# A two-layer encoder on one core: rows scaled before they are turned, and another order of loads in the opening

## The chip, the cores and the metric

One NeuronCore of one Trainium2 chip runs the whole program in one launch. The metric is the device time of an execution in microseconds (us). TensorE (PE) multiplies and turns tiles, VectorE (DVE) and ScalarE (ACT) work on elements, SyncE (SP) issues the loads from DRAM, GpSimd (POOL) does a few memsets.

## The reference, cut to what matters

Two sequences, 1024 rows ("sample") and 256 rows ("prompt") of 1024 features, go through two layers with the same weights. Only the start of the first layer matters here:

```python
for i in range(DEPTH):
    mod = jax.nn.silu(c) @ w_ada[i] + b_ada[i]
    sh1, sc1, g1, sh2, sc2, g2 = jnp.split(mod[:, None, :], 6, axis=-1)
    h = rms_norm(x, norm_g[i, 0]) * (1 + sc1) + sh1
    ...                                   # GLA mixer: q, k, v, r, gates from h
    x = x + g1 * rms_norm(y, norm_g[i, 1])
    h = rms_norm(x, norm_g[i, 2]) * (1 + sc2) + sh2
    ...                                   # SwiGLU FFN
def rms_norm(x, g):
    return x * lax.rsqrt(jnp.mean(x * x, axis=-1, keepdims=True) + EPS) * g
def gla_mixer(h, w_in, w_gk1, ...):
    q, k, v, r = jnp.split(h @ w_in, ...)
    gate = jnp.einsum('bld,edr->eblr', h, w_gk1)
    ...
```

## The kernel before, in words

The rows are cut into three blocks: C (the 256 prompt rows), A and B (512 sample rows each). Everything is fp32; a product is made in three passes over a rounded part and a remainder (`hhi`/`hlo` for activations, `uhi`/`ulo` for weights), and the activations stand with the features on the partitions, as eight pieces `k` of 128 features.

The opening stage runs from the start of the program to the loop over heads. Its parts, with the names used below:

- `rows1`/`rows2`: seven small loads (conditioning vectors, norm gains, biases), turned by PE into `vec1`/`vec2`; `sct` is silu of the conditioning vectors.
- `load_x` (L657, L662, L663) loads tiles of 128 rows (`xtok`, 512 KB), PE turns each in eight 128x128 transposes, and DVE or ACT copies the turned halves from PSUM into `xt`.
- `squares`, `rstd_of`, `newton` (L443 to L465): squares of the turned block summed over the eight pieces on DVE, a matmul with `ones_d` that sums over partitions, and a Newton step on the block's whole width give `r`, the reciprocal root of each row's mean square, in every partition.
- `ada_group` (L338, L348): the shift and scale vectors come from `w_ada`, in two halves of four pieces each. A half needs eight loads of 512 KB (`wada`) and two matmuls per load. `ada_out` (L394, L412, L422, L430) brings the sums into `mods`.
- `apply_norm` (L481, L482, L492): per piece `u` = `xt` x scale x `r` (DVE), `hhi` = round(`u` + shift) (ACT), `hlo` = `u` + shift - `hhi` (DVE).
- `products`: the gate rank products (`gk1`, L734, L735) and the first head's q and k (`mm3`, L307 to L309) of C and A, in two halves that follow the two halves of `mods`. Later `vproj` (L322) makes the first head's values of C and A, while `norm_b` squares, scales and splits block B; then come `gk1` and q, k of B, and the values of B (L322 at 108.17 us).

Three things set the order. Each engine has one stream of instructions, written out by a scheduler in the build from the program's order, the data and its own times; on the chip an engine that waits holds up all behind it. SP's stream is the queue of the loads. And a load needs a free buffer: `rawp` has three of 512 KB for row tiles and weights, `up` five `uhi` and five `ulo`, which `wada` shares with split weights.

Of the kernel before, what the change touches and what calls it, by code (L numbers as in the profile page):

```python
# [8 lines left out]
F32 = mybir.dt.float32  # L9
# [3 lines left out]
ALU = mybir.AluOpType  # L13
# [4 lines left out]
KD = 8  # L18
# [20 lines left out]
def encoder_kernel(  # L39
# [400 lines left out]
    def sq_add(acc, a, k, p):  # L440
        n = a.shape[-1]
        if k == 0:
            act.activation(acc, a, AF.Square)  # L443
        else:
            sq = p.tile([128, n], F32, tag="sq", name=nm("sq"))
            act.activation(sq, a, AF.Square)
            dve.tensor_add(acc, acc, sq)

    def rstd_of(acc, n, p, ones=ones_d, exp=False):
        ms = ps_ax()[:, :n]  # L450
        pe.matmul(ms, lhsT=ones, rhs=acc, start=True, stop=True)
        return newton(ms, n, p, exp)
# [15 lines left out]
    def col(md, v, cd, k):  # L468
        return md[:, v, cd, k : k + 1]

    last_hi = [None]

    def apply_norm(blk, L, first, xt, r, keep=None, ks=range(KD)):
        n, cd, f = BLK[blk], COND[blk], BLK[blk] / 512
        md = mods[L]
        vsh, vsc = (0, 1) if first else (3, 4)
        last = None
        for k in ks:
            sh = col(md, vsh, cd, k)
            u = xt[:, k, :] if keep is None else keep.tile([128, n], F32, tag="u", name=nm("u"))  # L480
            dve.scalar_tensor_tensor(out=u, in0=xt[:, k, :], scalar=col(md, vsc, cd, k), in1=r, op0=ALU.mult, op1=ALU.mult)  # L481
            last_hi[0] = act.activation(hhi[blk][:, k, :], u, AF.Identity, bias=sh)  # L482
            yield 0.66 * f
            if last is not None:
                lo_part(blk, *last)
                yield 0.66 * f
            last = (k, u, sh)
        lo_part(blk, *last)
        yield 0.66 * f

    def lo_part(blk, k, u, sh):
        dve.scalar_tensor_tensor(  # L492
            out=hlo[blk][:, k, :], in0=u, scalar=sh, in1=hhi[blk][:, k, :].bitcast(F32), op0=ALU.add, op1=ALU.subtract,
        )


    def square_sum(to, a):
        act.activation(bt.tile([128, 512], F32, tag="sq", name=nm("sq")), a, AF.Square, accum_out=to)
# [1 line left out]
    def sums_tile(blk, tag):  # L500
        return bt.tile([128, BLK[blk] // 128, 2], F32, tag=tag + blk, bufs=1, name=nm("ss"))

    def rstd_tok(ss):
        nt = ss.shape[1]
        m, r, t = [bt.tile([128, nt], F32, tag=x, name=nm(x)) for x in ("m", "rt", "tt")]
# [4 lines left out]
        dve.tensor_mul(t, m, t)  # L510
        dve.tensor_scalar(t, t, -0.5, 1.5, ALU.mult, ALU.add)
        dve.tensor_mul(r, r, t)
        return r
# [113 lines left out]
        vs[blk] = v  # L627

    with tc.tile_pool(name="st", bufs=1, reuse_waits="tile") as st:
        rows1 = st.tile([98, 128], F32)  # L630
        rows2 = st.tile([96, 128], F32)
        ngr = norm_g.rearrange("l s (k p) -> (l s k) p", p=128)
        dma(out=rows1[V_C : V_C + 8, :], in_=c_sample.rearrange("a (k p) -> (a k) p", p=128))
        dma(out=rows1[V_C + 8 : V_C + 16, :], in_=c_prompt.rearrange("a (k p) -> (a k) p", p=128))
        dma(out=rows1[V_NG : V_NG + 64, :], in_=ngr)
        dma(out=rows1[V_GK : V_GK + 8, :], in_=gla_b_gk[0].rearrange("e (h p) -> (e h) p", p=128))
        dma(out=rows1[V_SGB : V_SGB + 8, :], in_=sg_b_in[0, 0:1024].rearrange("(k p) -> k p", p=128))
        dma(out=rows1[V_GH : V_GH + 2, :], in_=gla_g_head[0].rearrange("(k p) -> k p", p=128))
        dma(out=rows2, in_=b_ada.rearrange("l (k p) -> (l k) p", p=128))
        pt = ps_ax()  # L640
        pe.transpose(pt[:, 0:98], rows1, ident[:98, :98])
# [4 lines left out]
        act.activation(sct, vec1[:, V_C : V_C + 16].rearrange("p (c k) -> p c k", c=2), AF.Silu)  # L646

        xt = {}
        def load_x(blk, tiles=None, bank=ps_mm):
            n = BLK[blk]  # L650
            if blk not in xt:
                xt[blk] = st.tile([128, KD, n], F32, tag="xt" + blk, name=nm("xt"))
            t = xt[blk]
            s, o = src[blk]
            for i in tiles or range(n // 128):
                a = rawp.tile([128, D], F32, tag="raw", name=nm("xtok"))
                dma(out=a, in_=s[o + i * 128 : o + (i + 1) * 128, :])  # L657
                for hf in range(2):
                    ps = bank()
                    for j in range(4):  # L660
                        k = 4 * hf + j
                        pe.transpose(ps[:, j * 128 : (j + 1) * 128], a[:, k * 128 : (k + 1) * 128], ident)  # L662
                    (act.copy if hf or blk == "B" else dve.tensor_copy)(  # L663
                        t[:, 4 * hf : 4 * hf + 4, i * 128 : (i + 1) * 128], ps.rearrange("p (j t) -> p j t", j=4)
                    )

        class STP:
            def tile(self, shape, dt, tag, name):
                return st.tile(shape, dt, tag=tag, bufs=3 if tag == "r" else 2, name=name)

        stp = STP()

        accs = {}

        def norm_b():
            n = BLK["B"]
            acc = st.tile([128, n], F32, tag="accB", bufs=1, name=nm("acc"))
            for k in range(KD):
                sq_add(acc, xt["B"][:, k, :], k, stp)
                yield 0.6  # L680
            yield 0.6
            r = rstd_of(acc, n, stp)
            yield 2.3
            yield from apply_norm("B", 0, True, xt["B"], r, stp)

        def squares(blk):
            accs[blk] = st.tile([128, BLK[blk]], F32, tag="acc" + blk, bufs=1, name=nm("acc"))
            for k in range(KD):
                sq_add(accs[blk], xt[blk][:, k, :], k, stp)

        class ADP:
            i = 0
# [2 lines left out]
                self.i += 1  # L695
                return up.tile(shape, dt, tag=("uhi", "ulo")[self.i % 2], name=name)

        rs = {}
        adp = ADP()
        adas = [ada_group(0, (0, 1), adp, "wada", None, half=i) for i in range(2)]  # L700

        def ada_n(i, n=99):
            for _ in range(n):
                if next(adas[i], None) is None:
                    break
# [10 lines left out]
        act.copy(g1v[:, :, :, 2, :], g1v[:, :, :, 0, :].bitcast(F32))  # L716
        act.copy(g1v[:, :, :, 3, :], g1v[:, :, :, 1, :].bitcast(F32))

        load_x("C")
        ada_n(0, 2)  # L720
        load_x("A", [0, 1])
        squares("C")
        ada_n(0, 2)
        load_x("A", [2, 3])
        ada_n(0, 3)
        rs["C"] = rstd_of(accs["C"], BLK["C"], stp)
        squares("A")
        rs["A"] = rstd_of(accs["A"], BLK["A"], stp)
        ada_n(0)

        def gk1(ps, blk, ks=range(KD)):
# [28 lines left out]
                tick(us_, rate)  # L760

        halves = (range(0, 4), range(4, KD))
        acc_ps = {"C": [p[:, :256] for p in (ps_mm(False), ps_mm(False), ps_ax())], "A": [ps_so() for _ in range(2)]}

        def products(i, blk, n=0):
            ps = acc_ps[blk]
            gk1(ps[0], blk, halves[i])
            ada_n(1, n)
            for p, w in zip(ps[1:], (wq, wk)):
                mm3(p, w, blk, halves[i])  # L770
                ada_n(1, n)
            if i == 1:
                gk1_out(ps[0], blk)
                q_out(ps[1], blk)
                if blk == "A":
                    ps.append(ps_mm(False))
                    mm3(ps[2], wk, blk)
                k_out(ps[2], blk)

        def norm(blk, i):  # L780
            for _ in apply_norm(blk, 0, True, xt[blk], rs[blk], stp, halves[i]):
# [961 lines left out]
```

## Time and profile before

| | |
|---|---|
| median of 3 runs | 2790.86 us (2787.03 to 2794.0) |
| the profiled execution | 2796.02 us, span 2794.3 us |
| PE busy | 2724.6 us, 98% of the span |
| DVE, ACT, POOL busy | 1740.7, 1118.2, 32.6 us |
| DMA | 410.41 MB, mean 147 GB/s |
| mean granted TensorE clock | 0.990 |

The profile divides the span into 40 slices of 70 us, with tenths of busy time; 9 is 90% or more. PE is at 9 nearly everywhere: it is the bound of the program, and what is not busy lies at the start, at the end and in short waits. The opening stage is the first slice and a half.

### The profile page before, as it was taken

Reading aid. Unit: us, or ns where it says so; the run is one execution under the profiler, and the core shown is the slowest. Engines: PE = TensorE matmul, PEld = TensorE weight load, DVE = VectorE, ACT = ScalarE, POOL = GpSimd, SP = SyncE. Lnnn points to the kernel's source line nnn. Section 1 sums busy time; section 2 is a strip of 40 time slices with the busy share of each in tenths; the row PEclk is TensorE's granted clock in tenths of the full one; section 3 lists DMA queues with packets and bytes.
Section 4 is the critical chain, followed back from the end, with each engine's and each line's share of the span. In section 5 each row is a group of like instructions: output and inputs, shape, how many; then the busy total and the mean of one; then the engine's idle time right before and its main releaser. Section 6 shows DMA issues by size and latency. Waiting matters only on the chain.

```text
span 2794.3 us, 37049 instructions
## 1 busy us (share of the span) xinstructions
PE 2724.6 (98%) x14208; PEld 2280.7 (82%) x14208; DVE 1740.7 (62%) x2749; ACT 1118.2 (40%) x1892; POOL 32.6 (1%) x47
## 2 busy tenths in 40 slices
PE   7999999999999999999999999999999999999998
PEld 4887888977888788888778868887887888888886
DVE  6763646587865654447778578666856554445576
ACT  5442434444622223224357344425422232234443
POOL 0000000000000000000000000000000000000000
PEclk9999999999999999999999999999999999999999
DMA  6224232155255542237877342334355532237676
GB/s 231 68 67 149 74 110 69 54 177 180 96 165 172 180 138 76 96 97 259 267 245 240 125 158 77 121 125 148 100 166 176 187 98 92 79 115 260 195 235 210
DMA packets 317542, 410.41 MB, mean 147 GB/s; under 512 B 21058, under 2 KB 194820, under 8 KB 317364
## 3 DMA queue, kind: packets, MB, share of 16 engines
q1 hardware_dynamic: 317364, 408.04, 44.9%
q8 instruction: 111, 1.82, 0.3%
q14 instruction: 67, 0.55, 0.1%
HBM read 304.65 MB, written 103.32 MB: 146 GB/s over the span
## 4 chain that ended last, share of the span: by engine, by line
PE 73%; DMA 12%; DVE 10%; issue 2%; ACT 1%; SPq 1%; POOL 0%; DVEq 0%; ACTq 0%; POOLq 0%
PE pso L1260 11%; PE pmm L1260 5%; PE pmm L322 4%; DMA y<-in_ffn_w_out_dram 3%; PE pax L1260 3%; PE pso L1434 2%; PE pso L1435 2%; PE pso L1436 2%; DMA raw<-in_ffn_w_in_dram 2%; PE pmm L309 2%; PE pmm L308 2%; PE pmm L307 2%; PE pax L307 2%; PE pax L308 2%; PE pax L309 2%
## 5 line engine op out<-in xcount | busy, mean ns | idle before, releaser
L145 ACT CAST uhi<-raw 128x1024 fp32r<-128x1024 f32 (+1 forms) x299 | 307.5, 1030 | 640.6 <-issue 283.3
L146 DVE TENSOR_TENSOR ulo<-raw,uhi 128x1024 fp32r<-128x1024 f32 (+1 forms) x299 | 357.1, 1196 | 236.0 <-ACT uhi L145 231.9
L309 PE MATMUL pax<-hhiC,ulo 128*128 128x256 f32 x680 | 192.6, 283 | 0.0
L307 PE MATMUL pax<-hhiC,uhi 128*128 128x256 f32 x680 | 192.5, 283 | 0.0
L308 PE MATMUL pax<-hloC,uhi 128*128 128x256 f32 x680 | 192.4, 283 | 0.0
L1260 PE MATMUL pso<-t,uhi 128*128 128x512 f32 x428 | 150.4, 413 | 21.8 <-DVE c L1337 21.7
L1434 PE MATMUL pso<-uhi,hhiB 128*128 128x512 f32 x374 | 145.7, 390 | 1.0 <-DVE y L1417 1.0
L1435 PE MATMUL pso<-uhi,hloB 128*128 128x512 f32 x374 | 145.6, 389 | 0.0
L1436 PE MATMUL pso<-ulo,hhiB 128*128 128x512 f32 x374 | 145.5, 389 | 0.0
L307 PEld LDWEIGHTS pax<-hhiC,uhi 128*128 128x128 f32 x680 | 130.3, 192 | 3.8 <-ACT v L580 0.4
L308 PEld LDWEIGHTS pax<-hloC,uhi 128*128 128x128 f32 x680 | 130.2, 191 | 3.1
L309 PEld LDWEIGHTS pax<-hhiC,ulo 128*128 128x128 f32 x680 | 130.2, 191 | 1.7 <-issue 1.7
L1382 ACT CAST hhiB<-tl 128x512 fp32r<-128x512 f32 x154 | 94.5, 619 | 87.0 <-PE pso L1436 33.9
L1383 DVE TENSOR_TENSOR hloB<-tl,hhiB 128x512 fp32r<-128x512 f32 x154 | 105.6, 700 | 36.4 <-ACT hhiB L1382 36.1
L1260 PEld LDWEIGHTS pso<-t,uhi 128*128 128x128 f32 x428 | 81.8, 198 | 40.4 <-DVE c L1337 24.2
L1260 PE MATMUL pso<-y,uhi 128*128 128x512 f32 x324 | 109.2, 391 | 0.0
L173 DVE TENSOR_TENSOR y<-raw 128x512 f32<-128x512 f32 x40 | 27.6, 691 | 111.8 <-DMA raw<-in_ffn_w_in_dram 111.8
L1434 PE MATMUL pmm<-uhi,hhiB 128*128 128x512 f32 x242 | 94.5, 391 | 0.0
L1436 PE MATMUL pmm<-ulo,hhiB 128*128 128x512 f32 x242 | 94.2, 389 | 0.0
L1435 PE MATMUL pmm<-uhi,hloB 128*128 128x512 f32 x242 | 94.2, 389 | 0.0
L371 DVE SCALAR_TENSOR_TENSOR aacc<-wada,sct,aacc 128x1024 f32<-128x1024 f32 x70 | 87.6, 1278 | 8.2 <-DMA wada<-in_w_ada_dram 8.2
L1260 PE MATMUL pmm<-hloA,uhi 128*128 128x512 f32 x216 | 84.3, 390 | 0.0
(470 smaller groups left out, 7292.2 us busy)
## 6 DMA issues: line engine op xcount, KB each, us to landing
wada<-in_w_ada_dram SPq DMA_DIRECT2D x96, 512.0 KB
raw<-in_ffn_w_in_dram SPq DMA_DIRECT2D x88, 512.0 KB
tl<-tdr SPq DMA_DIRECT2D x154, 256.0 KB
raw<-in_ffn_w_out_dram SPq DMA_DIRECT2D x74, 512.0 KB
y<-in_ffn_w_out_dram SPq DMA_DIRECT2D x88, 256.0 KB
sdr<-y SPq DMA_DIRECT2D x44, 512.0 KB
raw<-sdr SPq DMA_DIRECT2D x40, 512.0 KB
tdr<-c SPq DMA_DIRECT2D x60, 256.0 KB
```

The source lines that it names most:

```text
L145: act.copy(hi[:, :n], raw[:, :n])
L146: dve.tensor_sub(lo[:, :n], raw[:, :n], hi[:, :n].bitcast(F32))
L307: pe.matmul(ps, lhsT=hi[:, c], rhs=hhi[blk][:, k, :], start=(k == 0), stop=False)
L308: pe.matmul(ps, lhsT=hi[:, c], rhs=hlo[blk][:, k, :], start=False, stop=False)
L309: pe.matmul(ps, lhsT=lo[:, c], rhs=hhi[blk][:, k, :], start=False, stop=(k == KD - 1))
L322: pe.matmul(ps, lhsT=l, rhs=r, start=(i == 0), stop=(i == 3 * KD - 1))
L1260: pe.matmul(ps, lhsT=l[:, c], rhs=r[:, k, :], start=start, stop=(k == 3 and l is lo), skip_group_check=True)
L1382: act.copy(hi, t)
L1383: dve.tensor_sub(lo, t, hi.bitcast(F32))
L1434: pe.matmul(ps, lhsT=th[:, t], rhs=hi[:, c], start=(k == 0), stop=False)
L1435: pe.matmul(ps, lhsT=tl[:, t], rhs=hi[:, c], start=False, stop=False)
L1436: pe.matmul(ps, lhsT=th[:, t], rhs=lo[:, c], start=False, stop=(k == NK - 1))
```

## The change

It touches the opening stage, and leaves the rest of the program's text as it is.

- A row tile is scaled before it is turned: `turn_x` squares the tile as loaded (two ACT instructions with a running sum per row), makes the reciprocal root on one number per row (`rstd_tok`), multiplies the tile in place (one DVE instruction of 128x1024), and only then turns it. The sums over pieces, the matmul with `ones_d` and the Newton step on the block's width fall away, for A, B and C.
- `mod_x` takes the place of `apply_norm`: ACT makes `hhi` straight from `xt`, DVE makes `u` = `xt` x scale + shift, and `hlo` = `u` - `hhi`.
- Loads: C's two row tiles stand first, then all eight `wada` of the first half (`ahead` 7), then `gk1`'s weights. The seven small loads are issued by ACT. A's row tiles come after the q and k weights, and are turned behind C's first products. The first value weights are loaded ahead of B's last two row tiles.

```diff
-    def rstd_tok(ss):
+    def rstd_tok(ss, p=None):
...
+        adas = [ada_group(0, (0, 1), adp, "wada", None, ahead=(7, 4)[i], half=i) for i in range(2)]
...
+        def load_x(blk, i):
+            a = xin[blk, i] = rawp.tile([128, D], F32, tag="raw", name=nm("xtok"))
+            dma(out=a, in_=rows_of(src, blk, i, slice(0, D)))
+        def turn_x(blk, i, bank=ps_mm):
+            a = xin.pop((blk, i))
...
+            for hf in range(2):
+                act.activation(st.tile([128, 512], ...), a[:, halves_of(hf)], AF.Square, accum_out=ss[:, 0, hf : hf + 1])
+            dve.tensor_scalar(a, a, rstd_tok(ss, st), None, ALU.mult)
+            for hf in range(2):
+                ps = bank()
+                for j in range(4):
+                    k = 4 * hf + j
+                    pe.transpose(ps[:, j * 128 : (j + 1) * 128], a[:, k * 128 : (k + 1) * 128], ident)
+                (act.copy if hf or blk == "B" else dve.tensor_copy)(xt[blk][...], ps...)
+        def mod_x(blk, ks=range(KD)):
+            for k in ks:
...
+                last_hi[0] = act.activation(hi, x, AF.Identity, bias=sh, scale=sc)
+                u = stp.tile([128, n], F32, tag="u", name=nm("u"))
+                dve.tensor_scalar(u, x, sc, sh, ALU.mult, ALU.add)
+                yield 0.6 * f
+                dve.tensor_sub(hlo[blk][:, k, :], u, hi.bitcast(F32))
+                yield 0.7 * f
+        for i in range(2):
+            load_x("C", i)
+        ada_n(0, 1)
...
+        adma = act.dma_start
+        adma(out=rows1[V_C : V_C + 8, :], in_=c_sample...)      # and the six others
...
-        load_x("C")
-        ada_n(0, 2)
-        load_x("A", [0, 1])
-        squares("C")
-        ada_n(0, 2)
-        load_x("A", [2, 3])
-        ada_n(0, 3)
-        rs["C"] = rstd_of(accs["C"], BLK["C"], stp)
-        squares("A")
-        rs["A"] = rstd_of(accs["A"], BLK["A"], stp)
+        for i in range(2):
+            turn_x("C", i)
         ada_n(0)
...
         norm("C", 0)
         wq, wk = units.next(("q", 0), 1), units.next(("k", 0), 0)
+        for i in range(3):
+            load_x("A", i)
+        products(0, "C")
+        for i in range(4):
+            turn_x("A", i, ps_so)
+            if i == 0:
+                load_x("A", 3)
+                ada_n(1, 1)
         norm("A", 0)
-        ada_n(1, 5)
-        products(0, "C", 2)
-        load_x("B", [0], ps_so)
-        products(0, "A", 2)
-        load_x("B", [1], ps_so)
+        products(0, "A")
+        ada_n(1, 9)
+        for i in range(2):
+            load_x("B", i)
+        turn_x("B", 0, ps_so)
         ada_n(1)
         norm("C", 1)
         norm("A", 1)
+        units.ahead(1)
+        for i in (2, 3):
+            load_x("B", i)
         products(1, "C")
-        load_x("B", [2, 3], ps_so)
+        turn_x("B", 1, ps_so)
         products(1, "A")
-        gen_b = vec.push(norm_b())
+        for i in (2, 3):
+            turn_x("B", i, ps_so)
+        gen_b = vec.push(mod_x("B"))
         wv0 = [units.next(("v", 0, i), 1 - i) for i in range(2)]
```

What the scheduler makes of it, at three places. First SP's queue at its start; `xtok` are row tiles, `raw` of `gla_w_gk` is `gk1`'s weight, and the number behind a name is its buffer. Before:

```order
L639 DMA rows_155<-in_b_ada_dram 96x128
L712 DMA raw_171<-in_gla_w_gk_dram 128x8x16 x2
L657 DMA xtok_179<-in_x_prompt_dram 128x1024
L657 DMA xtok_193<-in_x_prompt_dram 128x1024
L338 DMA wada_208<-in_w_ada_dram 128x2x512
L338 DMA wada_212<-in_w_ada_dram 128x2x512
L657 DMA xtok_215<-in_x_sample_dram 128x1024
L657 DMA xtok_229<-in_x_sample_dram 128x1024
L338 DMA wada_268<-in_w_ada_dram 128x2x512
L338 DMA wada_272<-in_w_ada_dram 128x2x512
```

SP's queue after the change starts with C's two row tiles and the eight `wada` of the first half in a row; its end and what follows:

```order
L338 DMA wada_171<-in_w_ada_dram 128x2x512
L338 DMA wada_173<-in_w_ada_dram 128x2x512
L691 DMA raw_192<-in_gla_w_gk_dram 128x8x16 x2
L134 DMA raw_303<-in_gla_w_in_dram 128x8x128
L134 DMA raw_309<-in_gla_w_in_dram 128x8x128
L632 DMA xtok_315<-in_x_sample_dram 128x1024
L338 DMA wada_388<-in_w_ada_dram 128x2x512
L632 DMA xtok_317<-in_x_sample_dram 128x1024
L632 DMA xtok_319<-in_x_sample_dram 128x1024
```

Six of the first half's `wada` have moved ahead of A's tiles, and A's first tile now stands behind the q and k weights (`raw_303`, `raw_309`).

Second, ACT's stream at its start, after the change (before, it begins with the casts of `g1hi`, and its first three table loads stand ahead of a cast, of `sct` and of the block-wide `r`):

```order
L677 DMA rows_176<-in_b_ada_dram 96x128
L641 ACT_TABLE_LOAD
L641 ACTIVATE sq_201,ss_200<-xtok_154 128x512
L641 ACTIVATE sq_203,ss_200<-xtok_154 128x512
L641 ACTIVATE sq_229,ss_228<-xtok_156 128x512
L485 ACT_TABLE_LOAD
L485 ACTIVATE rt_206<-m_205 128x1
L641 ACTIVATE sq_231,ss_228<-xtok_156 128x512
L684 ACT_TABLE_LOAD
L684 ACTIVATE sct<-vec_85 128x16
L485 ACT_TABLE_LOAD
L485 ACTIVATE rt_234<-m_233 128x1
```

Four table loads stand there now: ahead of the first square, of each of the two roots (`rt`) and of `sct`.

Third, PE's stream around the last `wada` of the second half; L348 is the matmul with `wada`, L412 the turning of its sums, `pso_379`/`pso_380` A's products, `pmm_376` C's. Before:

```order
L348 MATMUL pax_425<-wada_474,sct 2x512 x2
L309 MATMUL pax_378<-hhiC_92,ulo_406 128x256
L734 MATMUL pso_379<-hhiA_90,g1hi_170 128x512
L735 MATMUL pso_379<-hloA_93,g1hi_170 128x512
L734 MATMUL pso_379<-hhiA_90,g1hi_170 128x512
L735 MATMUL pso_379<-hloA_93,g1hi_170 128x512
L734 MATMUL pso_379<-hhiA_90,g1hi_170 128x512
L735 MATMUL pso_379<-hloA_93,g1hi_170 128x512
L412 MATMUL pax_494<-ident,adar_490 128x64 x4
L734 MATMUL pso_379<-hhiA_90,g1hi_170 128x512
L735 MATMUL pso_379<-hloA_93,g1hi_170 128x512
L307 MATMUL pso_380<-hhiA_90,uhi_399 128x512
```

After (`pso_498`/`pso_499` are A's products, `pmm_321` to `pax_323` C's):

```order
L309 MATMUL pso_499<-hhiA_90,ulo_306 128x512
L348 MATMUL pax_387<-wada_530,sct 2x512
L647 MATMUL pso_567<-ident,xtok_546 128x128 x4
L647 MATMUL pso_573<-ident,xtok_546 128x128 x4
L412 MATMUL pax_579<-ident,adar_542 128x64 x4
L705 MATMUL pso_498<-hhiA_90,g1hi_191 128x512
L307 MATMUL pso_499<-hhiA_90,uhi_305 128x512
L705 MATMUL pmm_321<-hhiC_92,g1hi_191 128x256
L307 MATMUL pmm_322<-hhiC_92,uhi_305 128x256
```

Before, the twenty products of A's first half and one of C's follow the last matmul with `wada` and come ahead of C's second half; after the change A's first half is already done there, and one turned tile of B, the turning of the sums and two products stand between. Behind the opening the engines' streams are the same apart from two things: the first layer's output projection and the normalization that follows it (L1146, L547 and L572 of the profile, around 600 us) are interleaved somewhat differently, and since `ps_mm` is called eight times fewer, the PSUM banks that later calls get are shifted in their round of five.

More of the change, by code (lines that the diff above doesn't have):

```diff
@@ L471, in encoder_kernel @@
     last_hi = [None]
[L473 to L494, printed above, removed]
     def square_sum(to, a):
@@ L501, in sums_tile @@
         return bt.tile([128, BLK[blk] // 128, 2], F32, tag=tag + blk, bufs=1, name=nm("ss"))
-    def rstd_tok(ss):
+    def rstd_tok(ss, p=None):
         nt = ss.shape[1]
-        m, r, t = [bt.tile([128, nt], F32, tag=x, name=nm(x)) for x in ("m", "rt", "tt")]
+        m, r, t = [(p or bt).tile([128, nt], F32, tag=x, bufs=2, name=nm(x)) for x in ("m", "rt", "tt")]
         dve.tensor_add(m, ss[:, :, 0], ss[:, :, 1])
@@ L629, in encoder_kernel, with tile @@
     with tc.tile_pool(name="st", bufs=1, reuse_waits="tile") as st:
+        class STP:
+            def tile(self, shape, dt, tag, name):
+                return st.tile(shape, dt, tag=tag, bufs=2, name=name)
+        stp = STP()
+        class ADP:
+            i = 0
+            def tile(self, shape, dt, tag, bufs, name):
+                self.i += 1
+                return up.tile(shape, dt, tag=("uhi", "ulo")[self.i % 2], name=name)
+        adp = ADP()
+        adas = [ada_group(0, (0, 1), adp, "wada", None, ahead=(7, 4)[i], half=i) for i in range(2)]
@@ new lines, in ada_n @@
+        def ada_n(i, n=99):
+            for _ in range(n):
+                if next(adas[i], None) is None:
+                    break
+        xt, xin = {}, {}
+        def load_x(blk, i):
[3 more added lines that the diff above has]
+            a = xin.pop((blk, i))
+            if blk not in xt:
+                xt[blk] = st.tile([128, KD, BLK[blk]], F32, tag="xt" + blk, name=nm("xt"))
+            ss = st.tile([128, 1, 2], F32, tag="ss", bufs=2, name=nm("ss"))
+            for hf in range(2):
+                act.activation(st.tile([128, 512], F32, tag="sq", bufs=2, name=nm("sq")), a[:, halves_of(hf)], AF.Square, accum_out=ss[:, 0, hf : hf + 1])
+            dve.tensor_scalar(a, a, rstd_tok(ss, st), None, ALU.mult)
[4 more added lines that the diff above has]
+                    pe.transpose(ps[:, j * 128 : (j + 1) * 128], a[:, k * 128 : (k + 1) * 128], ident)
+                (act.copy if hf or blk == "B" else dve.tensor_copy)(
+                    xt[blk][:, 4 * hf : 4 * hf + 4, i * 128 : (i + 1) * 128], ps.rearrange("p (j t) -> p j t", j=4)
+                )
@@ new lines, in mod_x @@
+        def mod_x(blk, ks=range(KD)):
+            n, cd, f = BLK[blk], COND[blk], BLK[blk] / 512
+            for k in ks:
+                sc, sh = col(mods[0], 1, cd, k), col(mods[0], 0, cd, k)
+                x, hi = xt[blk][:, k, :], hhi[blk][:, k, :]
+                last_hi[0] = act.activation(hi, x, AF.Identity, bias=sh, scale=sc)
[4 more added lines that the diff above has]
+                yield 0.7 * f
@@ L646, in encoder_kernel @@
         act.activation(sct, vec1[:, V_C : V_C + 16].rearrange("p (c k) -> p c k", c=2), AF.Silu)
[L648 to L692, printed above, removed]
-            def tile(self, shape, dt, tag, bufs, name):
[L695 to L705, printed above, removed]
         g1hi = up.tile([128, 1024], F32R, tag="uhi", name=nm("g1hi"))
@@ L762, in encoder_kernel, with products @@
         halves = (range(0, 4), range(4, KD))
-        acc_ps = {"C": [p[:, :256] for p in (ps_mm(False), ps_mm(False), ps_ax())], "A": [ps_so() for _ in range(2)]}
-        def products(i, blk, n=0):
+        acc_ps = {}
+        def products(i, blk):
+            if blk not in acc_ps:
+                acc_ps[blk] = [p[:, :256] for p in (ps_mm(False), ps_mm(False), ps_ax())] if blk == "C" else [ps_so(), ps_so()]
             ps = acc_ps[blk]
             gk1(ps[0], blk, halves[i])
-            ada_n(1, n)
             for p, w in zip(ps[1:], (wq, wk)):
                 mm3(p, w, blk, halves[i])
-                ada_n(1, n)
             if i == 1:
@@ L780, in norm @@
         def norm(blk, i):
-            for _ in apply_norm(blk, 0, True, xt[blk], rs[blk], stp, halves[i]):
+            for _ in mod_x(blk, halves[i]):
                 pass
```

14 lines of the change are left out of this document (7 added, 7 removed).

## Prediction

> **What bounds the kernel now.** First the page: the span, PE's busy tenths in slices of 70 us, the granted clock.
>
> ```profile
> span 2794.3 us, 37049 instructions
> PE   7999999999999999999999999999999999999998
> PEclk9999999999999999999999999999999999999999
> ```
>
> PE is the bound everywhere but in the first and last slice, so a microsecond saved on PE's way through the opening is a microsecond of the span, unless a later stage waits for something that does not move. The windows of the opening (length, busy us of PE, PEld, DVE, ACT, POOL with counts, clock, DMA share, GB/s) say where PE loses time.
>
> ```profile
> 0.00:20.00 20.00, 10.47 (x52) 6.21 (x52) 6.41 (x14) 10.33 (x20) 1.50 (x12) 1.00 0.79 274
> 20.00:40.00 20.00, 13.94 (x57) 5.89 (x56) 15.46 (x31) 11.77 (x19) 0.00 (x0) 0.74 0.88 294
> 52.60:108.20 55.60, 55.52 (x337) 47.89 (x337) 41.60 (x69) 28.17 (x47) 3.52 (x9) 1.00 0.22 64
> 28.00:30.00 2.00, 0.00 (x0) 0.00 (x0) 1.79 (x3) 1.83 (x3) 0.00 (x0) 0.87 1.12 342
> 42.00:44.00 2.00, 2.00 (x10) 0.36 (x8) 1.87 (x4) 1.38 (x2) 0.00 (x0) 0.72 0.28 108
> ```
>
> In the first 40 us PE is busy 24.4 us, some of it at half clock; from 52.6 us to 108.2 us, where the values of B begin, it is busy 55.52 of 55.60 us at full clock. So the question is at what time the changed kernel reaches the state that before has at 52.6 us, and whether PE then runs as densely. The clock fell to half inside the window from 28 us and was back inside the one from 42 us.
>
> The timeline of PE, SP and ACT in the opening gives the prices (start, duration, engine, line, count):
>
> ```profile
> 0.80 0.41 SPq L633 DMA_DIRECT2D rows<-in_c_sample_dram  x1
> 3.05 0.25 SPq L638 DMA_DIRECT2D rows<-in_gla_g_head_dram  x1
> 4.44 0.40 PE L641 MATMUL pax<-ident,rows 98*128 98x98 f32 x1 [4.44 <-DMA rows<-in_gla_g_head_dram]
> 4.80 1.05 SPq L657 DMA_DIRECT2D xtok<-in_x_prompt_dram  x2
> 8.24 1.28 ACT L646 ACT_TABLE_LOAD   x1
> 8.92 1.11 PE L662 MATMUL pmm<-ident,xtok 128*128 128x128 f32 x4 [3.37 <-DMA xtok<-in_x_prompt_dram]
> 9.53 0.22 ACT L646 ACTIVATE sct<-vec 128x16 f32<-128x16 f32 x1
> 9.83 2.74 PE L662 MATMUL pso<-ident,xtok 128*128 128x128 f32 x12
> 24.94 1.03 PE L348 MATMUL pax<-wada,sct 128*2 128x512 f32 x4 [0.32 <-DMA wada<-in_w_ada_dram]
> 26.33 1.03 PE L348 MATMUL pax<-wada,sct 128*2 128x512 f32 x4 [0.36 <-DMA wada<-in_w_ada_dram]
> 30.23 2.07 PE L451 MATMUL pax<-acc,ones_d 128*128 128x512 f32 x2 [2.88 <-DVE acc L447]
> 36.20 1.88 PE L348 MATMUL pax<-wada,sct 128*2 128x512 f32 x4
> 38.88 0.58 PE L734 MATMUL pmm<-hhiC,g1hi 128*128 128x256 f32 x1 [0.81 <-ACT hhiC L482]
> 52.15 0.68 DVE L394 COPY adar<-pax 2x512 f32<-2x512 f32 x1 [4.82 <-PE pax L348]
> 54.77 0.88 DVE L481 SCALAR_TENSOR_TENSOR u<-xt,mods,r 128x256 f32<-128x256 f32 x2
> ```
>
> C's first product starts at 38.88 us. Loads of 512 KB arrive 1.39 us apart (24.94, 26.33). A transpose at half clock takes 2.74/12 = 0.23 us; one `wada` costs PE 1.88 us at half clock. From the copy of the sums to the first `u` it is 54.77 - 52.15 = 2.6 us. Full-clock prices stand in the chain of waits:
>
> ```profile
> 45.63 0.96 PE pax L348 x4
> 62.27 0.44 PE pso L662 x4
> 74.85 5.75 PE pmm L322 x48
> 80.61 0.86 PE pax L451 x2
> 81.46 11.51 PE pmm L322 x96
> 92.97 0.23 PE pmm L734
> 108.17 5.76 PE pmm L322 x48
> ```
>
> A `wada` is 0.96, eight transposes (a row tile) 0.88, a 256-wide product 5.75/48 = 0.12, a 512-wide one 0.23, the 64 products of B 108.17 - 92.97 = 15.2 us. The element work that the change puts on ACT and DVE is seen elsewhere in the program:
>
> ```profile
> 648.87 0.63 ACT L498 ACTIVATE sq<-y 128x512 f32<-128x512 f32 x1 [7.60 <-DVE y L547]
> 649.54 0.63 ACT L498 ACTIVATE sq<-y 128x512 f32<-128x512 f32 x1
> L510 DVE TENSOR_TENSOR tt<-m,tt x21: 151/161/166, 643.8 to 2785.1; 128x4 f32<-128x4 f32 x14, 128x2 f32<-128x2 f32 x7
> L560 DVE TENSOR_SCALAR y<-y,rt x30: 742/748/754, 661.3 to 1964.9; 128x1024 f32<-128x1024 f32 x30
> L464 DVE TENSOR_SCALAR t<-t x3: 293/426/426, 21.5 to 83.7; 128x512 f32<-128x512 f32 x2, 128x256 f32<-128x256 f32 x1
> 43.05 1.41 DVE L492 SCALAR_TENSOR_TENSOR hloA<-u,mods,hhiA 128x512 fp32r<-128x512 f32 x2
> 35.45 0.58 ACT L663 COPY xt<-pso 128x512 f32<-128x512 f32 x1 [0.75 <-PE pso L662]
> 42.30 1.38 ACT L482 ACTIVATE hhiA<-u,mods 128x512 fp32r<-128x512 f32 x2 [1.22 <-DVE u L481]
> 30.70 1.20 DVE L146 TENSOR_TENSOR ulo<-raw,uhi 128x1024 fp32r<-128x1024 f32 x1
> ```
>
> A half of squares with its sum is 649.54 - 648.87 = 0.67 us, a small DVE step 0.16 (about 0.2 with the gap to the next, an estimate), the scaling 0.75, an ACT copy 0.58, `hhi` 0.69, `u` 0.29 or 0.43, `hlo` 0.7, the split of a weight on DVE 1.2.
>
> **The change, step by step: up to C's first product.** SP issues C's tile at 0.80 instead of 4.80. From issue to use it was 4.1 us (4.80 to 8.92) behind the small loads; a small load takes 1.4 us (3.05 to 4.44), and with 1.3 for the bytes it is 2.7: the tile is there at 3.5 to 4.9. ACT issues seven small loads first. No trace shows ACT issuing one: at SP's pace (0.80 to 3.30 for six) the seventh, which waits for the sixth to land, is out at 4.8. If it cost nothing ACT would wait for the tile, 3.5 at best (1.3 us earlier); at twice SP's price it is 7.3 (2.5 later). I take SP's price, the nearest row. Then ACT: table load 1.28, three squares 2.0, table load 1.28, root 0.2, to 9.6. DVE: four small steps 0.8, one more 0.2, scaling 0.75, to 11.3. PE turns C's first tile cold, 8 x 0.23 = 1.8, to 13.1. `sct` needs `vec1`, whose copy stands behind that scaling, and a table load: 13.1 too. The `wada` are no limit: issued from 3.5 on, the eighth is there at 6.2 + 7 x 1.39 = 15.9, before PE asks for it. PE: first `wada` 1.9 (cold), one and a half more 1.45, C's second tile 0.9, five and a half `wada` 5.3: 22.7. Then 2.6 us to `u`, and one weight split (1.2) that DVE's stream puts between the two gain steps: `hhiC` at 26.5, first product at 27.0, 11.9 us earlier than 38.88.
>
> [...]
>
> **To A's first product.** The 32 products of C's first half cost 3.8 us at full clock and 7.7 at half; PE has been idle for 4 us before them, and `hloC` comes from DVE until about 30.4. They end between 32.8 (full clock from 31) and 34.7 (half throughout); I take 33.5. Half a `wada` and A's first tile: 34.9. Here is what the lead is paid back with: A's fourth tile gets its buffer only now. Load 2.7, to 37.7, but ACT first copies the third tile, whose scaling DVE reaches at 38 (0.7 for a copy, then two tiles' small steps and scalings, 2.9), so its squares start at 39.6: 1.35, steps and root 1.3, scaling 0.75, transposes 0.9, to 44.0; copy and the larger part of a first `hhi` 1.1: A's first product at 45.1. PE has the other seven `wada` and two tiles in these 10 us, work for 8.5 at full clock, so this hides nothing more.
>
> **From there to B's values.** The 55.6 us from 52.6 on are my measure: there C's first half is done and five products of A are. At 45.1 the changed kernel still has those five (1.15), one more tile of B (0.88) and half a `wada` (0.48), and lacks B's matmul with `ones_d` (0.86): 57.25 us. Extra waits: A's first half paced by DVE (`u` 0.43 + `hlo` 0.7 per piece, two `u` ahead) 0.7; behind the last `wada` PE has one tile, the turning of the sums and two products, while the sums go through DVE, ACT, PE and DVE with B's scaling, a copy and the value weights' split among them, 2.5 us idle; A's second half 0.5; B's last two tiles, scaled after both tiles' roots, 1.3. Sum 5.0. The 55.6 already hold such waits: listed work is 59 x 0.23 + 3.8 + 2.6 + 0.4 + 17.3 + 0.9 + 15.2 = 53.8, so 1.8 us; the extra is 3.2. B's values begin at 45.1 + 57.25 + 3.2 = 105.5 instead of 108.2: **2.7 us earlier**. B's own split (8 x 1.15 us of DVE) has the 17.3 us of `vproj` to hide in; without that cover it would cost 9. The value weights, ahead of B's last tiles, are split long before `vproj`: no gain, since before they were there at 74.85 without a wait.
>
> **Behind the opening** the streams are the same but for the first output projection. There PE waited:
>
> ```profile
> PE pax L572 <- DVE y L560: 6.0, 2, 4.6
> ```
>
> Its new interleaving can take some of these 6.0 us away or add as much; the shifted banks can do a little of either. I count 0, from -6 to +6. Against the profiled execution (2796.02 us) this is 2793.3; it ran 5.2 above the median of the three runs, so for the median 2790.86 - 2.7 = **2788.2**. A difference under 0.3%, 8.4 us, is about what a measurement of this kernel cannot tell from no change.
>
> **Rivals.** (1) The lead survives. If PE's queue covers the extra 3.2 us, and C's first half runs warm from 31 (0.7) and ACT's small issues are hidden (1.3), the opening gains 7.9; with the longest wait of the output projection (4.6) gone it is 12.5, about 2778.5. For it: the 11.9 us at C's first product. Against it: the fourth tile's chain, which is all latency. (2) The clock, on the slower side. PE has two gaps of about 2 us, before A's last tile is turned and behind the last `wada`. Before, PE's work of 26.33 ended at 27.4, and the 0.87 of the window from 28 us puts the fall at 29.5: 2.1 us. It stayed at half until 43, although PE worked again from 34. If the first gap makes it fall and it stays at half until A's second half is done, the 40 + 32 products cost 9.4 + 3.8 us more, less the 2.7: 2801. It decides from gaps of 2.1 us on. (3) The change moves waits without removing any: ACT's issues at twice SP's price (2.5) eat the gain, and the time is 2791, not to be told from before.
>
> [...]
>
> **How the numbers follow.** Forecast (opening 0 to 8 us shorter or a few longer, rest as before) 0.54; rival 1 0.23; rival 2 0.14; rival 3 0.09. Faster by over 0.3%: rival 1 and a rest of the forecast, 0.25; slower: rival 2, 0.14; within: 0.61. The range takes in the forecast with -6 and +6 from the output projection, most of rival 1 and part of rival 2: 2779 to 2799.
>
> **What would show it.** Right: C's first product near 27, A's near 45, a PE wait of 2 to 3 us behind the last `wada`, B's values (L322's third group) near 105.5. Wrong: the clock at half beyond 45 (rival 2); A's products before 42 or B's values before 101 (rival 1); the first squares later than 6.5 (rival 3); or a difference that lies near 600 to 700 us and not in the opening at all.

## The result, and the profile after

The changed kernel is slower. Its median is 2810.72 us (five runs, 2806.42 to 2821.6) against 2790.86; the ratio is 1.0065, 95% interval 1.0047 to 1.0082, so +18 us. Eight more runs gave 2804.2 us against 2790.47, ratio 1.0043 (1.0027 to 1.0058), +12 us. Both lie above the range on record, 2779 to 2799. The profiled execution took 2815.83 us, its span is 19.8 us longer than before's.

The page of the changed kernel: span, PE's tenths, granted clock.

```profile
span 2814.1 us, 37121 instructions
PE   7999999999999899999999999999999999999998
PEclk9999999999999999999999999999999999999999
```

At this grain nothing is seen but one 8 in the fourteenth slice. The windows of the opening (columns as before: length, busy us of PE, PEld, DVE, ACT, POOL, then clock, DMA share, GB/s):

```profile
0.00:20.00 20.00, 10.37 (x40) 3.90 (x42) 4.89 (x18) 9.45 (x17) 1.50 (x12) 1.00 0.88 281
20.00:40.00 20.00, 15.50 (x82) 9.72 (x78) 12.63 (x42) 11.31 (x27) 0.00 (x0) 0.83 0.81 268
40.00:60.00 20.00, 16.45 (x71) 7.57 (x70) 12.79 (x36) 11.87 (x24) 0.52 (x1) 1.00 0.60 200
60.00:80.00 20.00, 18.95 (x109) 16.59 (x108) 15.13 (x42) 13.63 (x33) 3.32 (x9) 0.91 0.17 56
```

PE gains 1.6 us of busy time between 20 and 40 us, and at a better clock (0.83 against 0.74). But from 40 to 80 us, where before ran dense, 4.6 us are idle and the clock falls once more. Rows of the timelines of SP and PE, and the group of the products that start B's values:

```profile
27.36 0.58 PE L705 MATMUL pmm<-hhiC,g1hi 128*128 128x256 f32 x1 [2.58 <-ACT hhiC L657]
36.34 0.34 SPq L632 DMA_DIRECT2D xtok<-in_x_sample_dram  x1
37.25 4.72 SPq L338 DMA_DIRECT2D wada<-in_w_ada_dram  x4
46.78 1.03 PE L348 MATMUL pax<-wada,sct 128*2 128x512 f32 x4 [0.48 <-DMA wada<-in_w_ada_dram]
48.23 1.02 PE L348 MATMUL pax<-wada,sct 128*2 128x512 f32 x2 [0.41 <-DMA wada<-in_w_ada_dram]
49.18 0.50 PE L705 MATMUL pso<-hhiA,g1hi 128*128 128x512 f32 x1
56.22 0.66 PE L647 MATMUL pso<-ident,xtok 128*128 128x128 f32 x4 [0.68 <-ACT xt L648]
58.77 0.50 PE L705 MATMUL pso<-hhiA,g1hi 128*128 128x512 f32 x1 [1.49 <-ACT hhiA L657]
L322 PE MATMUL pmm<-uhi,hhiB x128: 277/283/388, 110.8 to 506.8; 128*128 128x256 f32 x128
```

C's first product comes at 27.36 us, 11.5 earlier than before. A's first comes at 49.18, behind `wada` that land late: SP issued A's fourth row tile at 36.34 and the last four `wada` only behind it. B's values begin at 110.8 us instead of 108.0. So the opening itself lost 2.8 us in this execution.

The larger part arises behind it. First before, then the changed kernel, at the end of the loop over heads (L958 and L942, L960 and L944 are its products into `pso`; L1146 and L1130 the first output projection; L925 and L909 a step of the head loop):

```profile
555.24 0.40 PE L1146 MATMUL pmm<-uhi,hhiC 128*128 128x512 f32 x1
555.97 0.49 PE L958 MATMUL pso<-p,v 128*128 128x128 f32 x2
557.21 0.58 PE L1146 MATMUL pmm<-uhi,hhiC 128*128 128x512 f32 x1
562.85 1.90 PE L925 MATMUL pax<-qx,kk 128*128 128x64 f32 x16
573.26 0.48 PE L1146 MATMUL pso<-uhi,hhiC 128*128 128x512 f32 x1
```

```profile
559.06 0.49 PE L942 MATMUL pso<-p,v 128*128 128x128 f32 x2 [0.56 <-DVE S L935]
562.26 0.49 PE L942 MATMUL pso<-p,v 128*128 128x128 f32 x2 [1.61 <-DVE S L935]
565.08 0.67 PE L1130 MATMUL pmm<-uhi,hhiA 128*128 128x512 f32 x1 [1.66 <-ACT hhiA L570]
566.40 3.52 PE L909 MATMUL pax<-qx,kk 128*128 128x64 f32 x16
```

Before, products of the projection's first C tile, in a bank `pmm`, stand between the head loop's steps and cover them; the second C tile, in a `pso`, starts only at 573.26, when the head loop has left that ring. After the change no C product stands there: the first product of the projection is one of A, in a `pmm`. PE waits three times, 3.8 us together: twice for `S` (the running state of the head, made by DVE at L935) and once for A's rounding. Then it runs at half clock: sixteen instructions of L909 take 3.52 us instead of 1.90.

### The profile page after: what moved, and what is told of

It is laid out like the page before. It is cut to its first block, busy times and chain, and to the rows that moved or that the text cites. A ratio compares the mean times of both kernels' runs of the same rounds, so it can differ in the third digit from the quotient of the medians.

```text
span 2814.1 us, 37121 instructions
## 1 busy us (share of the span) xinstructions
PE 2728.5 (97%) x14202; PEld 2285.5 (81%) x14202; DVE 1732.8 (62%) x2786; ACT 1119.4 (40%) x1914; POOL 33.3 (1%) x47
## 4 chain that ended last, share of the span: by engine, by line
PE 71%; DMA 13%; DVE 10%; issue 2%; ACT 1%; SPq 1%; POOL 0%; ACTq 0%; DVEq 0%; POOLq 0%
PE pso L1244 10%; PE pmm L1244 5%; PE pmm L322 4%; DMA y<-in_ffn_w_out_dram 4%; DMA sdr<-y 2%; PE pax L1244 2%; PE pso L1420 2%; PE pso L1419 2%; PE pso L1418 2%; PE pmm L307 2%; PE pmm L308 2%; PE pmm L309 2%; DVE ulo L146 2%; DMA raw<-in_ffn_w_in_dram 2%; PE pso L1132 2%
## 5 line engine op out<-in xcount | busy, mean ns | idle before, releaser
L1418 PEld LDWEIGHTS pso<-uhi,hhiB 128*128 128x128 f32 x374 | 70.5, 188 | 17.6 <-DVE y L1401 1.5
```

Of the source, the lines that this page charges most:

```text
L1418: pe.matmul(ps, lhsT=th[:, t], rhs=hi[:, c], start=(k == 0), stop=False)
```

## The experiments

Two theories stood against each other. P: the round of the banks makes the loss behind the opening. `ps_mm` counts its calls. Where the caller allows both kinds, a call whose count, divided by 5, leaves 2 or more gets a bank of the `so` ring, and the others one of the two `mm` banks. The change makes eight calls fewer, so every later call stands at another place of the round of five. Before, C's two tiles of the first projection had counts that leave 1 and 2 (`mm`, `so`); after the change they leave 3 and 4 (`so`, `so`), and A's first two tiles get the `mm` banks. S: the loss follows from the changed opening itself. The table has all runs; the columns behind the ratio are how many us a kernel's profile lags behind before's profile at five places: the start of B's values (108.0), the last of A's values (492.2), the head loop's last product (573.2), the first transposes behind the projection (662.1), the last products of the program (2782.0). Profiles are single executions: the 31 runs of before that stand beside e5 to e8 spread from 2783.8 to 2798.3 us, and before's profiled execution took 5.2 us more than its median. So differences of a few us in the last columns say little.

| kernel | median us | ratio to before (95%) | B's values | A's values | head loop | L572/L549 | end |
|---|---|---|---|---|---|---|---|
| changed | 2810.72 | 1.0065 (1.0047 to 1.0082) | 2.8 | 3.1 | 7.2 | 13.9 | 19.7 |
| e1 old round, new opening | 2796.64 | 1.0021 (1.0011 to 1.0031) | -0.1 | -0.7 | -0.7 | -2.3 | -1.9 |
| e2 new round, old opening | 2797.82 | 1.0029 (1.0016 to 1.0042) | -0.1 | 0.0 | 4.0 | 8.9 | 4.2 |
| e3 changed, round +1 | 2798.56 | 1.0027 (1.0015 to 1.0039) | 1.0 | 1.2 | 1.2 | -1.5 | 1.2 |
| e4 changed, round +4 | 2802.51 | 1.0044 (1.0029 to 1.0059) | 0.1 | 0.2 | 4.2 | 10.0 | 5.6 |
| e5 changed again | 2804.2 | 1.0043 (1.0027 to 1.0058) | 1.5 | 0.8 | 4.9 | 10.1 | 6.8 |
| e6 round +2 in one stage | 2794.36 | 1.0009 (0.9997 to 1.0021) | 2.5 | 2.6 | 2.6 | 0.8 | -0.6 |
| e7 changed, round +2 | 2794.16 | 1.0008 (0.9997 to 1.002) | 3.4 | 3.3 | 3.3 | 0.9 | 8.4 |
| e8 before, round +4 | 2789.39 | 0.9992 (0.998 to 1.0003) | -0.9 | -0.7 | -0.7 | -1.6 | -5.4 |
| e9 e6, buffer for A's 4th tile | 2791.8 | 1.0006 (0.9995 to 1.0016) | -0.9 | 0.0 | 0.0 | -2.1 | 2.9 |
| e10 e6, sums under A's products | 2791.48 | 1.0 (0.9991 to 1.001) | -2.7 | 0.5 | 0.5 | -1.2 | -2.0 |
| e11 e9 and e10 | 2790.96 | 1.0004 (0.999 to 1.0018) | -3.5 | -0.2 | -0.2 | 0.6 | 2.4 |
| e12 e11, gate rows on DVE | 2782.24 | 0.9974 (0.996 to 0.9987) | -3.7 | -4.4 | -4.4 | -6.8 | -17.1 |

### e1 to e4: the round of the banks

e1 sets the count back to before's round; e3 and e4 are the same line with 1 and 4; e2 puts `ps_mm.i += 2` behind the loads of A's row tiles in the kernel before.

```diff
         for i in range(2):
             turn_x("C", i)
+        ps_mm.i += 3
         ada_n(0)
```

> The changed kernel with the count of ps_mm set forward by 3 behind C's row tiles, so that each later call gets the PSUM bank of the round that it had before. Every engine's stream behind the opening then reads as before's, bank names included; the opening stays the changed one. Theory P (the round of banks makes the loss behind the opening): what is left is the opening's own +2.8 us (B's values at 110.8 instead of 108.0), so about 2793.6, between 2790 and 2797, 17 us under the changed kernel. Rival S (the loss follows from the changed opening itself, through times of loads, the clock or which buffers rotate): the time stays near 2810.7, between 2806 and 2815.

> The kernel before with the count of ps_mm set forward by 2 at the end of its opening, so that all later calls get the banks that they get in the changed kernel; the opening stays before's. Theory P: the whole loss without the new opening, 2790.9 + 17 = about 2808, between 2803 and 2812. Rival S: no difference, 2791, between 2788 and 2794.

> The changed kernel with the count of ps_mm set forward by 1. The streams of DVE, ACT and SP and the order of work at the first output projection are then as before's (but for two products that change places), the banks of the later calls are in a third position. Theory P, if the order at the first output projection makes the loss: near 2794 to 2800. Theory P, if the banks of the later stages (the FFN's products) make most of it: anywhere from 2790 to 2812, apart from e1 by more than 4 us. Rival S: 2810.

> The changed kernel with the count of ps_mm set forward by 4. The streams of DVE, ACT and SP are word for word the changed kernel's, PE's but for twelve instructions of the first output projection; the banks of the later calls are in another position. Theory P, if the order at the first output projection makes the loss: within 3 us of the changed kernel, 2808 to 2814. Theory P, if the later banks make most of it: apart from it by more than 4 us. Rival S: 2810.

P holds in kind, in both directions: e1 takes away 12 of the 18 us (2796.64, within the stated 2790 to 2797; against the second measurement of the changed kernel, e5, it is 7.6 us), and e2 makes the kernel before 8 us slower (2797.82) with nothing else touched; that is less than the 17 expected, and below the stated 2803 to 2812. Its timeline has the changed kernel's three waits at the same instructions, number for number:

```profile
555.93 0.49 PE L959 MATMUL pso<-p,v 128*128 128x128 f32 x2 [0.56 <-DVE S L952]
559.13 0.49 PE L959 MATMUL pso<-p,v 128*128 128x128 f32 x2 [1.61 <-DVE S L952]
561.95 0.80 PE L1147 MATMUL pmm<-uhi,hhiA 128*128 128x512 f32 x1 [1.66 <-ACT hhiA L593]
563.39 3.52 PE L926 MATMUL pax<-qx,kk 128*128 128x64 f32 x16
```

The lags divide the kernels into two classes. Where a C tile has an `mm` bank (before, e1, e3), the lag does not change from 492 to 573 us and does not grow to the transposes; where both are on `so` (changed, e2, e4), it grows by about 4 there and by 9 to 11 up to the transposes. e3, with e1's order and other banks later on, is within 2 us of it. S is out for this part. Left open by these four: e4 came out at 2802.5, not at the 2808 to 2814 stated from the changed kernel's first runs, so either the later banks matter too, or the first runs of the changed kernel were long by chance.

### e5 to e8: the one stage, and the changed kernel again

e5 is the changed kernel. e6 shifts the round only for the first half of the first projection; all later calls have the changed kernel's banks. e7 shifts it for good (`ps_mm.i += 2` in the opening), e8 puts `ps_mm.i += 4` into the kernel before, at e2's place.

```diff
         for hf in range(2):
             ws = [units.next((tag, hf, i), (2, 1, 1, 0)[i]) for i in range(4)]
+            if L == 0:
+                ps_mm.i += (2, 3)[hf]
             for b in ORDER:
```

> The changed kernel once more, for a second profile of it beside the next three. If its loss over e4 (same streams behind the opening but for twelve instructions, 2802.5) belongs to the banks of its later stages, the time is again 2807 to 2815 and the first products of the FFN of layer 0 lag 11 us behind before's. If it was the chance of waits and clock in that execution (the clock at half from 60.0 to 63.4 us in the opening, longer waits for c in the FFN), this profile shows B's values near 108 to 109 instead of 110.8, and a span near that of e4, 2797 to 2806.

> The changed kernel with the count of ps_mm set forward by 2 for the first half of the first output projection only, and by 3 behind it, so that every later call has the changed kernel's bank again. C's two row tiles there then get banks of the mm pair instead of the so ring. Theory P1 (the loss behind the opening arises at that place: C's products, which are ready, have no bank while the head loop holds the so ring, so PE waits for S and for hhiA and the clock falls): PE's waits for S and hhiA at 555 to 562 us are gone, the first output product starts at 555 instead of 562 to 565, and the time falls 7 to 12 us under the changed kernel, to about 2800. Theory P2 (the banks of the later stages, the FFN's above all): no more than 4 us under it.

> The changed kernel with the count of ps_mm set forward by 2 for good: the same order of work as e6 on every engine, but other banks in all later stages. P1: as e6 within 4 us, and near e1 (2796.6), perhaps 1 us under it, since both of C's tiles now have a bank of the mm pair. P2: apart from e6 by more than 5 us.

> The kernel before with the count of ps_mm set forward by 4, so that both of C's tiles of the first output projection get a bank of the mm pair (before: the first one only). P1: PE had no wait there that this takes away, so the same as before within 3 us, 2788 to 2793; if the order it gives shortens the 6.0 us wait of the transposes behind the projection, up to 4 us faster. P2: anywhere from 2785 to 2800.

P1 is right and P2 falls. e6 is 9.8 us under e5 by the medians, and the banks of ten tiles, with the order that the build makes of them, are the only difference. PE's waits from 540 to 600 us, of the changed kernel and then of e6:

```profile
PE pso L942 <- DVE S L935: 2.2, 2, 1.6
PE pmm L1130 <- ACT hhiA L570: 1.7, 1, 1.7
PE pax L900 <- DVE kk L872: 0.4, 1, 0.4
```

```profile
PE pax L900 <- DVE kk L872: 0.4, 1, 0.4
```

e6's first product of the projection is one of C, in a `pmm`, at 557.88 us and without a wait:

```profile
557.88 0.40 PE L1130 MATMUL pmm<-uhi,hhiC 128*128 128x512 f32 x1
```

Between the last of A's values and the first product of the FFN (764.6 us in e6, 772.0 in e5), e5's profile falls 9.2 us further back than e6's, so the loss arises in this stretch. Each run also has its mean clock. What is missing to a full clock, times the run's time, is an estimate of the clock lost: it is 28.7 us on average in e5's runs and 22.3 in e6's, so 6.4 of the 10.2 us between their mean times are clock. e7, with other banks in every later stage, has e6's time within 0.2 us: the banks of the FFN show no cost, though either interval is 3.4 us wide to each side. e8 is as before within its interval. e5 shows that the first five runs of the changed kernel were on the long side: same program, 6.5 us less. In its profile the `c` wait of the FFN in layer 0 (750 to 1300 us) is 11.7 us where the first one had 15.0, before 10.8. (`c` is the FFN's intermediate result, which DVE makes.) What makes that wait longer in one execution than in another stays open.

### e9 to e11: why the opening lost its lead

With the projection mended, 2 to 3 us are left against before by e6 and e7 (6 to 8 by e1 and e3; the runs do not settle it closer), and the starts of B's values agree: over the seven profiles with the changed opening they come 1.6 us late on average (-0.1 to 3.4). e9 gives A's fourth row tile a buffer of its own:

```diff
-            a = xin[blk, i] = rawp.tile([128, D], F32, tag="raw", name=nm("xtok"))
+            pool_ = (st, dict(tag="x3", bufs=1)) if (blk, i) == ("A", 3) else (rawp, dict(tag="raw"))
+            a = xin[blk, i] = pool_[0].tile([128, D], F32, name=nm("xtok"), **pool_[1])
```

e10 writes the second half's last pieces ahead of A's products, e11 is both:

```diff
+        ada_n(1)
         products(0, "A")
-        ada_n(1, 9)
         for i in range(2):
             load_x("B", i)
         turn_x("B", 0, ps_so)
-        ada_n(1)
```

> e6, and A's fourth row tile gets a buffer of its own instead of the third of the raw ring. SP then issues all four A tiles and behind them the eight wada of the second half in one row; in e6 the fourth tile stands in SP's queue behind three of those wada and ahead of four, and waits there until A's first tile is turned (about 36 us). Theory Q1 (the opening lost its lead because the fourth tile's wait also held up the last wada: A's first product at 48 to 49 us instead of 45.1): A's first product moves to 45 to 46, B's values 2 to 3 us earlier than in e6 (110.5), the time 2 to 3 us under e6 (2794.4). Theory Q2 (the lead is lost in the gap behind the last wada and the fall of the clock that follows it): A's first product may move, but PE waits as much longer behind the last wada; B's values and the time within 1 us of e6.

> e6, with the last pieces of ada_group's second half written ahead of A's first-half products instead of behind them. The turning of the sums (L412) then stands between A's products in PE's stream, so these cover the copies and the steps to mods, and C's second half follows without the 2.2 us gap of before. Theory Q2: no PE wait of over 1 us between 50 and 62 us, the clock at full there, B's values 2 us earlier than in e6 if the clock doesn't fall in it, 4 us if it did (e6 110.5, so 106.5 to 108.5); the time 2 to 4 us under e6, about 2791. Theory Q1: the last wada now delay A's first products by as much as the gap was; B's values within 1 us of e6, time the same.

> e9 and e10 together. If both Q1 and Q2 hold, their gains add: A's first product at 45 to 46, no gap behind it, B's values at 103.5 to 106, which is 2 to 4 us ahead of the kernel before (107.1 to 108.0), and a time of 2786 to 2789, at the edge of what can be told from before (2790.4). If only one holds, near that one's time, 2790 to 2792.

Both Q1 and Q2 hold in the opening. SP's row and A's first product in e9 (in e6 at 48.98 us), then A's first product, the turned sums and B's first turned tile in e10:

```profile
27.25 14.63 SPq L338 DMA_DIRECT2D wada<-in_w_ada_dram  x8
43.75 0.50 PE L706 MATMUL pso<-hhiA,g1hi 128*128 128x512 f32 x1
```

```profile
48.24 0.50 PE L705 MATMUL pso<-hhiA,g1hi 128*128 128x512 f32 x1
51.87 0.46 PE L412 MATMUL pax<-ident,adar 64*128 64x64 f32 x4
54.65 0.63 PE L647 MATMUL pso<-ident,xtok 128*128 128x128 f32 x4 [0.34 <-DVE xtok L642]
```

e9's eight `wada` are issued in one row from 27 us, and A's products start 5.2 us earlier, more than the 3 expected; in e10 the products cover the turning of the sums (1.49 us of wait are gone), and the clock stays. B's values start 3.4, 5.2 and 6.0 us earlier than in e6. e9 keeps only 3.4 of its 5.2 because its clock is at half from 54.7 to 61.5 us (0.68, 0.50, 0.50 and 0.62 in the windows of 2 us from 54 to 62), which costs 3.4 us against 1.7 in e6. The times follow only in part: 2.6 to 3.4 us by the medians, 0.0003 to 0.0009 (0.8 to 2.5 us) by the ratios, which is within their intervals; all three are level with before, and e11 was expected at 2786 to 2789. At the last of A's values e10 and e11 are level with before again. Windows of before and then of e11:

```profile
260.00:270.00 10.00, 7.60 (x35) 5.35 (x35) 3.86 (x4) 3.26 (x4) 6.31 (x4) 1.00 0.60 173
270.00:280.00 10.00, 10.00 (x78) 9.51 (x77) 6.64 (x14) 8.18 (x16) 0.00 (x0) 1.00 0.61 184
```

```profile
260.00:270.00 10.00, 7.47 (x33) 6.40 (x32) 3.29 (x5) 2.99 (x5) 5.18 (x3) 0.80 0.54 164
270.00:280.00 10.00, 10.00 (x66) 9.32 (x65) 6.20 (x11) 7.94 (x16) 0.00 (x0) 0.86 0.39 116
```

PE idles there in both, but in e11 the clock falls behind it (0.80 and 0.86). These are 20 us at a mean of 0.83, so 3.4 us: the lead.

### e12: the place where the lead is given back

```diff
-                pool.tensor_tensor(row, row, more, op=ALU.add)
+                dve.tensor_tensor(row, row, more, op=ALU.add)
...
-                pool.tensor_tensor(row, row, more, op=ALU.mult)
+                dve.tensor_tensor(row, row, more, op=ALU.mult)
```

> e11, and the two additions and multiplications on ada_out's gate rows (L404, L406 of the profile, 2x512) run on DVE instead of POOL. e11 brought B's values 3.5 us ahead of the kernel before, and was level with it again at 492 us: at 266 us PE waits 2.5 us for POOL's L406, and the clock is at half from 266 to 273 us there, which costs another 3.4. Theory R1 (the opening's lead is given back at that place): with DVE (0.7 us an operation as in L394, against 1.3 to 2.1 of POOL) the wait is under 1 us, the clock stays, the last product of A's values (492.0 in e11) comes at 486 to 488, and the time is 4 to 6 us under e11, 2785 to 2787. Rival R2 (the wait is set by the two loads between the steps, not by POOL): PE still waits 2 us or more there, and the time is within 2 us of e11. The edit also shifts a few products at the first output projection, which can add or take 2 us.

e12 moves four steps on the gate rows from POOL, which does these beside its memsets, to DVE. PE's wait at this place in e11, and in e12:

```profile
266.19 1.11 PE L412 MATMUL pax<-ident,adar 128*128 128x128 f32 x4 [2.53 <-POOL adar L406]
```

```profile
265.45 0.63 PE L412 MATMUL pax<-ident,adar 128*128 128x128 f32 x4 [2.03 <-DVE adar L406]
260.00:270.00 10.00, 7.97 (x52) 6.74 (x51) 7.04 (x11) 5.75 (x10) 0.00 (x0) 1.00 0.49 143
```

The wait went only from 2.53 to 2.03 us, as R2 had it (the loads between the two steps stay), but in this profile the clock stays at full and the lead of 4.4 us lives on to 573 us, as R1 had it. One profile does not show that the edit keeps the clock: with POOL it stayed in ten of thirteen. The time is 2782.24 us: faster than the kernel before by 0.26% (0.13% to 0.40%), and 8.7 us under e11 by the medians, 8.4 by the ratios. This is more than the 4 to 6 expected. By the estimate used for e5 and e6, e11's runs lost 23.0 us of clock on average and e12's 19.2, so 3.8 of the 9.0 us between their mean times are clock. PE's waits for `y` at L549 are 4.7 us in all against 11.2 in e11's profile, an execution 7.2 us above e11's median; that the products which the edit moves at the projections did this is not shown. How the 8.7 us divide between the two places wasn't tried apart, nor was this edit on the kernel before, so that POOL's steps were what gave the lead back is likely and not shown.

## Why the prediction was wrong, step by step

- **"Behind the opening I count 0, from -6 to +6": this step failed.** It measured +10 us (e5 against e6; 4 of them are there by the head loop's end, the rest by the FFN's first product). I saw that the round of banks moves and priced it as "a little of either"; and I priced the new interleaving from the one wait that before shows there, 6.0 us at L572. What I did not list is the work that covered a wait which the profile of before therefore does not show: C's products in an `mm` bank, between the head loop's steps on the `so` ring. With that cover gone the place costs, in the changed kernel's first profile, 3.8 us of waits, 3.4 of half clock (6.8 us at half) and 1.8 more at L549 (7.8 us of waits against 6.0). Before's own rows say it: a product into `pmm` at 555.24, the next tile's into `pso` not before 573.26.
- **A's first product at 45.1: it came at 49.18 (48.08 to 49.18 in e1, e6 and the changed kernel).** The chain of the fourth tile was right almost to the tenth (turned at 44.28 against 44.0). The error was "this hides nothing more": in SP's queue four `wada` stand behind that tile, and I did not follow the queue past the instruction that waits. e9 shows the price, 5.2 us at A's first product.
- **C's first product at 27.0: right**, 27.36, in part by luck: PE turned C's first tile at 10.19 us, 1.1 earlier than counted, and then took 4.52 us, nearly twice the full-clock price, for the two and a half `wada` that were counted at 3.35. The gap behind the last `wada`: right, 2.2 us against 2.5.
- **Opening 2.7 us shorter: wrong by sign**, 2.8 longer in that profile and 1.6 on average. Of that profile's 5.3 us (110.8 against 105.5), 4.1 are there at A's first product and 1.2 behind it, where the clock fell. One term was misread: at 52.6 us before has two of A's products done (52.20 and 52.43), not five, so the sum was 0.7 us too long there.
- **Rival 2, the clock: it came, at a smaller size.** The clock fell behind the gap, in four of six profiles with this opening (0.97 from 55 to 110 us in the changed kernel, e5, e6 and e7, 1.00 in e1 and e4), but for 3.4 us, not to the end of A's second half: it cost 1.7 us, not 13.2. The larger fall was at the projection, where I had no gap.
- **"A difference that lies near 600 to 700 us and not in the opening at all"** was named as what would make the forecast wrong, and the greater part came just ahead of that and in it, from 555 us on.

## What to carry to other kernels

A stage that is shortened by some calls of a round-robin allocator shifts every later call: compare which buffers the later stages get, first of all where two stages overlap and one of them holds a ring, and give such tiles a buffer by name, not by count (here only the count was shifted). A wait that is absent from the profile before is often one that something covers; for each instruction that moves, ask what it covered. In a queue that is served in order, as SP's was here (four `wada` out from 37.25 us behind the waiting tile, in e9 all eight in a row from 27.25), price what stands behind the instruction that waits, not only its own chain.

## What the runs showed of the hardware

Whether an idle gap halves the clock is decided by more than its length. After waits of PE of 0.68 and 1.50 us at the same place, e1 kept the full clock, and after 0.68 and 1.49 the changed kernel lost it (clock is the third number from the end; first e1, then the changed kernel):

```profile
60.00:62.00 2.00, 2.00 (x18) 2.00 (x18) 2.00 (x6) 2.00 (x4) 0.63 (x2) 1.00 0.10 33
```

```profile
60.00:61.00 1.00, 1.00 (x7) 1.00 (x7) 1.00 (x4) 1.00 (x3) 0.00 (x0) 0.54 1.06 434
63.00:64.00 1.00, 1.00 (x9) 1.00 (x8) 1.00 (x3) 0.00 (x0) 0.00 (x0) 0.75 0.00 0
565.00:566.00 1.00, 0.92 (x4) 0.80 (x5) 1.00 (x3) 0.59 (x3) 0.00 (x0) 0.63 0.75 283
572.00:573.00 1.00, 1.00 (x6) 0.83 (x5) 0.00 (x0) 0.00 (x0) 0.00 (x0) 0.96 0.82 283
```

The windows between stand at 0.50, so a 0.54 means half clock from 60.08 on, and a 0.75 half clock until 63.5: the fall lasted 3.4 us. The other runs from 565.26 to 572.08, which is 6.8; before's fall in the opening, 29.5 to 43.1, is 13.6. They begin 1.3 us behind the end of a gap (58.77), 0.2 us behind one (565.08) and in the middle of one (27.36 to 30.23).

PE's wait for POOL near 266 us shows the same. The changed kernel waited 2.7 us there and had the full clock from 200 to 300 us; e10 waited 2.4 and lost it (wait, then that stretch; first the changed kernel, then e10):

```profile
PE pax L412 <- POOL adar L406: 2.7, 1, 2.7
200.00:300.00 100.00, 95.84 (x617) 76.54 (x616) 40.03 (x75) 32.45 (x66) 7.08 (x5) 1.00 0.41 132
```

```profile
PE pax L412 <- POOL adar L406: 2.4, 1, 2.4
200.00:300.00 100.00, 96.16 (x605) 77.09 (x605) 40.30 (x76) 30.52 (x64) 7.22 (x5) 0.97 0.37 122
```

Behind waits of 1.6 us e9 lost the full clock (0.98 over that stretch) and e1 and e5 kept it (1.00). So the prediction's "from gaps of 2.1 us on" does not hold in these runs: a gap of 2.7 us left the clock at full, and one of 1.6 did not. What decides is not shown: no run varied a gap alone.

For a forecast it means that in these runs a gap of about 2 us cost its length, and 1.7 or 3.4 us more where 3.4 or 6.8 us of half clock came behind it. The place in the program does not settle that: behind the POOL wait at 266 us the clock fell in three of thirteen profiles with waits of 1.6 to 2.7 us (e9, e10 and e11), at the projection with its three waits in a row in four of four (0.94 from 545 to 600 us in each).
